# A decoder trunk in three-pass float32r: the shift product, the mean's copy, the diagonals, the merge's loop order and the last residual

## The chip, the cores and the metric

The program runs on 1 core of one Trainium2 chip. The metric is device microseconds of one execution, given as the median of three runs. Five engines matter: TensorE (PE, and PEld for its weight loads), VectorE (DVE), ScalarE (ACT), GpSimd (POOL), and SyncE (SP), which issues most DMAs.

## The reference, cut to what matters

Two layers; each has three steps, and each step ends in a layer norm over 1024 features. There are 528 tokens (16 learned meta tokens and 512 others), all in float32.

```
for l in range(2):
    h = layer_norm(ALPHA * h + 0.5 * swiglu(h, ffn1_w_up[l], ffn1_w_down[l]), ...)
    h = layer_norm(ALPHA * h + hybrid_mixer(h, ...), ...)
    h = layer_norm(ALPHA * h + 0.5 * swiglu(h, ffn2_w_up[l], ffn2_w_down[l]), ...)
return h[:, N_META:]
```

`swiglu` has 2816 hidden features. The mixer sums two gated branches, a short convolution and causal latent attention with 8 heads, and projects the sum by `w_o`.

## The kernel before, in words

**Products.** A float32 product runs as three float32r passes (`mm3`, L90 to L93): every operand is split into a rounded part and a rest. For weights ACT makes the rounded part (L111) and DVE the rest (L114); for activations both are in `split` (L88). Features lie on the partitions and tokens on the columns, so one pass takes 256, 264 or 272 columns.

**Token ranges and stages.** Tokens are cut in two parts, FULL (256 and 272) or, from the second layer's mixer on, TRIM (256 and 256 without the meta tokens). A feed-forward step (`ffn`) goes over pairs of feature tiles in chunks; `up_seven` makes two tiles of the hidden layer with seven products of halves, and calls `mid[...]` between them, which runs the down products of the chunk before (`down_features`). PSUM has eight banks: in a feed-forward step four for `psum()` (tile ps) and four for `psum2()` (tile pf), in the mixer six and two.

**What sets the order.** The kernel is written in the order of the generators' `yield`s and calls; the framework then orders each engine's instructions by its own estimate of when operands are ready. The order on an engine is fixed at compile time, and each engine takes its instructions strictly in that order. A block `tc.issue_after(ins)` puts what is issued in it behind `ins`, on the engine of `ins`.

**The norm.** `Norm.shift_by` (L248 to L257) takes the mean over the first 128 features of each token: DVE casts r's first tile to bf16 (L253), PE multiplies it by ones (L254), ACT copies the result (L256), and POOL subtracts it from r (L561 in the feed-forward step, L1133 in the merge). In `down_features` this happens within chunk 0, as soon as feature tile m = 0 of a part is added to r (L558). `Norm.add` (L259) collects sums of r and of its squares on DVE and POOL. `Norm.run` (L273) takes token sums on PE (L206), computes variance and `rsqrt` in 14 small DVE operations (L282 to L285 and L225 to L234), and spreads two rows over the partitions: `spread` (L210) makes diagonal matrices, by ACT for the mean (L216) and by DVE for the deviation (L218), and PE multiplies them by ones (L219). ACT copies the mean out of PSUM (L289), POOL subtracts it from r in eight operations (L292), DVE scales (L300), and ACT and DVE write the next operands xh and xl (L302 to L306, L88). There are five norms of two parts each that go this way; the mixer's two RMS norms use `spread` as well (`third`, L838), eight spreads in all.

**The merge.** `merge` (L1104) multiplies the two branches (w_bc with yc, w_bm with ym) for two feature tiles at a time, then projects by w_o, first for token part 0, then for part 1 (`proj_o`). Each product is followed by DVE operations (L1123, L1125) and a split into mg.

**The last residual.** In the last feed-forward step tokens go back to the partitions (`down_tokens`, L583). `begin` (L606) rebuilds x as xh + xl on DVE (L615), transposes it on PE (L617), and ACT writes it, scaled, to r viewed as four contiguous token tiles of 1024 (L618). It starts behind `combos` (L328), where POOL forms sums and differences of r (L337) that are split by ACT and DVE. `end` normalises (L647, L652), and SP stores 128 x 512 pieces (L654).

Of the kernel before, what the change touches and what calls it, by code (L numbers as in the profile page):

```python
# [51 lines left out]
def trunk(ctx: ExitStack, tc: tile.TileContext, x, meta, f1_up, f1_dn, w_in, b_gate, conv_w, qn_g, w_uq,  # L52
          kvn_g, w_ukv, w_bc, w_bm, w_o, f2_up, f2_dn, ln_g, ln_b, rope, out):
    """Float32 products run as three passes of float32r: an operand is hi + lo, hi its value rounded to 12
    significant bits and lo the exact rest, and hi*hi + hi*lo + lo*hi are summed in PSUM. Activations lie with
    their features on the partitions."""
# [8 lines left out]
    @contextmanager  # L65
    def scratch(n, t):
        """The eight banks of PSUM, n for psum() and the others for psum2(), and t tiles in SBUF."""
        with tc.tile_pool(name="psp", bufs=1, space=bass.MemoryType.PSUM, reuse_waits="tile") as pool, \
                tc.tile_pool(name="tmp", bufs=t, reuse_waits="tile") as tp:
            banks.append((pool, n))  # L70
            tps.append(tp)
            yield
            banks.pop()
            tps.pop()
# [15 lines left out]
    def mm3(ps, lhs, rhs, first, last, more=False):  # L90
        PE.matmul(ps, lhsT=lhs[0], rhs=rhs[0], start=first, stop=False, skip_group_check=more)  # L91
        PE.matmul(ps, lhsT=lhs[0], rhs=rhs[1], start=False, stop=False, skip_group_check=more)  # L92
        PE.matmul(ps, lhsT=lhs[1], rhs=rhs[0], start=False, stop=last, skip_group_check=more)  # L93
# [4 lines left out]
    def unit(pool=wp, k=8, c=P):  # L98
        """A stationary operand, hi and lo, as [128, k, c]."""
# [8 lines left out]
    def operand(raw, pool=wp, cut=1):  # L108
        """Split, in parts where others would wait for long."""
# [21 lines left out]
    # per-feature parameters as columns  # L131
# [11 lines left out]
    def tokens_in(xt, c0):  # L143
        """Two tiles of tokens, to the columns from c0."""
# [14 lines left out]
    with tc.tile_pool(name="xload", bufs=1, reuse_waits="tile") as xp, scratch(4, 1):  # L159
# [8 lines left out]
        # the array's clock falls while it waits for the first products' operands: of no use but for that  # L168
# [3 lines left out]
    def rest_in(pool):  # L172
        """The other tokens, and the parameters."""
# [21 lines left out]
    # Per-token statistics are taken with the tokens on the partitions, n of them in each of nt columns, and  # L195
    # spread back over the partitions of the features.
# [5 lines left out]
    def token_sums(ps, at, parts, n, nt):  # L202
        """Columns at, at + 2, ...: the means over D features of the parts together."""
# [6 lines left out]
    def spread(c, n, nt, act, ps):  # L210
        """c / D on all partitions."""
        ps = ps[:, :n * nt]
        for i in range(nt):
            dg = tmp(n)[0:n]
            if act:
                S.activation(dg, idf[0:n, 0:n], AF.Copy, scale=c[:, i:i + 1])  # L216
            else:
                V.tensor_scalar(dg, idf[0:n, 0:n], c[:, i:i + 1], None, op0=ALU.mult)  # L218
# [3 lines left out]
    def rsqrt(v, n, nt, by=float(D)):  # L222
        """by/sqrt(v): the exponent trick, a Newton step, and a step of third order."""
# [10 lines left out]
        V.tensor_tensor(y, u, y, op=ALU.mult)  # L234
        return y

    class Norm:
        """Layer norm over the features of r, which holds twice the sum to norm. The sums of r and of its squares
        are taken as its last parts come; by then r has been moved by a value near the mean of each token, which
        keeps the variance exact."""  # L240
# [7 lines left out]
        def shift_by(self, q0, w, i):  # L248
            """The mean of the first features of each token, on all partitions: near the mean, so that a rounded
            one does."""  # L250
            ps = psum()[:, :w]
            b = tmp(w).bitcast(BF16)[:, :w]
            V.tensor_copy(b, r[:, 0, q0:q0 + w])  # L253
            PE.matmul(ps, lhsT=onesb, rhs=b, start=True, stop=True)  # L254
            s = self.sums_tile(i, w)
            S.copy(s, ps)  # L256
            return s  # L257
# [15 lines left out]
        def run(self, q0, w):  # L273
            """The rest, in steps between which the tensor engine should have something else to do."""
# [11 lines left out]
            y = rsqrt(v, n, nt)  # L286
            yield
            mean = tmp(w)
            S.copy(mean, spread(mud, n, nt, True, psum2()))  # L289
# [4 lines left out]
            y = spread(y, n, nt, False, psum2())  # L294
# [24 lines left out]
    def project_steps(ps, u, nk, rhs, q0, w, n=4):  # L319
        """The same, with a stop after each n of the products' parts."""  # L320
# [7 lines left out]
    def combos(hv, th, tl):  # L328
        """Sums and differences of the parts of x (halves of its features, 1 and 2, and of its tokens, A and B)
        that the seven products take, split, from r that holds x. By index: T1 = x1B - x1A,  # L330
        T2 = x2B - T1, T3 = x2B - x1B, -T4 = x2A - T2."""
# [8 lines left out]
    def up_start(hp, dp, w_up, hv, pending, th, tl, after, begin):  # L340
        """silu(gate) * up for the first two pairs of feature tiles. What the first tokens allow comes first."""
# [62 lines left out]
    def up_seven(hp, fp, w_up, f, hv, mid, th, tl):  # L404
        """silu(gate) * up for two feature tiles by seven products of halves (Winograd's form): rows are gate and
        up, the contraction is halved, columns are the two token ranges."""
# [20 lines left out]
        product(pa, operand(g1), x1a, True)              # M1  # L427
# [28 lines left out]
        product(pc, operand(s1), t1, True)               # M5  # L456
        if mid[2]:
            mid[3]()
        for j in range(2):
            V.tensor_tensor(u3s[j], pc[j], u3s[j], op=ALU.add)   # up B  # L460
        if not mid[2]:
            mid[1]()
        product(pc, operand(g2, wp, 2), x2b, False)             # M5 + M3
        if mid[2]:
            mid[3]()
        for j in range(2):
            hh, hl = hs[j]
            V.tensor_tensor(u2s[j], pc[j], u2s[j], op=ALU.add)   # gate B
# [76 lines left out]
    def down_features(hv, norm):  # L545
        def down(ci, hs, mp, u, part):
            q0, w = hv[part]
            n = len(hs)
            for j in range(2):
# [3 lines left out]
                for k in range(n):  # L553
                    mm3(ps, [t[:, j * P:(j + 1) * P] for t in u[k]], [t[:, q0:q0 + w] for t in hs[k]],
                        k == 0, k == n - 1)
                if ci == 0:
                    rm = r[:, m, q0:q0 + w]
                    V.scalar_tensor_tensor(rm, rm, ALPHA2, ps, op0=ALU.mult, op1=ALU.add)  # L558
                    if m == 0:
                        shifts[part] = norm.shift_by(q0, w, part)  # L560
                    G.tensor_tensor(rm, rm, shifts[part], op=ALU.subtract)  # L561
# [17 lines left out]
        shifts = {}  # L579
# [3 lines left out]
    def down_tokens(l):  # L583
        """The last step's down products, with tokens on the partitions, and its norm."""
        rt = r.rearrange("p k t -> p (k t)")[:, 0:4 * D].rearrange("p (i d) -> p i d", d=D)

        def make(dp):
            state = {}

            def down(ci, hs, mp, u, part, tiles=None):  # L590
                last = ci == len(CHUNKS) - 1
                for i in tiles or (2 * part, 2 * part + 1):
# [5 lines left out]
                    rm = rt[:, i, mp * 256:(mp + 1) * 256]  # L598
                    V.tensor_tensor(rm, rm, ps, op=ALU.add)  # L599
# [6 lines left out]
            def begin():  # L606
                """The residual, token tile by token tile, where the features' x was."""
                for i in range(4):
                    t0 = META + i * P
                    for half in range(2):  # L610
                        ps = psum2()
                        for kk in range(4):
                            k = half * 4 + kk
                            xf = tmp(P)
                            V.tensor_tensor(xf, xh[:, k, t0:t0 + P].bitcast(F32),  # L615
                                            xl[:, k, t0:t0 + P].bitcast(F32), op=ALU.add)
                            PE.transpose(ps[:, kk * P:(kk + 1) * P], xf, idf)  # L617
                        S.activation(rt[:, i, half * 512:(half + 1) * 512], ps, AF.Copy, scale=ALPHA2)  # L618
# [17 lines left out]
            def end(tiles):  # L636
                """The norm of some tiles up to the scaling by the deviation, which is returned."""
# [6 lines left out]
                y = rsqrt(v, P, n, 1.0)  # L644
                halves = [(j, i, slice(c * 512, (c + 1) * 512)) for j, i in enumerate(tiles) for c in range(2)]
                for j, i, cs in halves:
                    V.scalar_tensor_tensor(rt[:, i, cs], rt[:, i, cs], mv[:, 2 * j:2 * j + 1], gb[0][:, cs],  # L647
                                           op0=ALU.subtract, op1=ALU.mult)

                def finish():  # L650
                    for j, i, cs in halves:
                        V.scalar_tensor_tensor(rt[:, i, cs], rt[:, i, cs], y[:, j:j + 1], gb[1][:, cs],  # L652
                                               op0=ALU.mult, op1=ALU.add)
                        nc.sync.dma_start(out[0, i * P:(i + 1) * P, cs], rt[:, i, cs])  # L654
# [19 lines left out]
    def gate(l, hv, wi, i, m2, dst, ps_of):  # L674
        """tanh of half the gates' arguments of two feature tiles: sigmoid(z) = (tanh(z / 2) + 1) / 2."""
# [523 lines left out]
```

## Time and profile before

| what | value |
|---|---|
| median of 3 runs | 2246.11 us (2245.96 to 2246.87) |
| profiled execution, span | 2247.7 us |
| PE busy / PEld busy | 2202.0 us (98%) / 2181.9 us (97%) |
| DVE / ACT / POOL busy | 1679.5 us (75%) / 974.5 us (43%) / 372.6 us (17%) |
| mean granted TensorE clock | 0.990 |

The profiled execution's own time is known by its span, from the first to the last instruction; it is 1.6 us above the median of the runs. Matmuls are pipelined: one is busy some 280 ns, and the next starts some 120 ns after it, so that the count of matmuls in a stretch tells more than the busy share.

### The profile page before, as it was taken

What the parts mean: (1) busy time and instruction counts of PE and PEld (TensorE: products, weight loads), DVE (VectorE), ACT (ScalarE), POOL (GpSimd) and SP (SyncE); (2) the same over time, 40 slices, a digit from 0 to 9 for tenths busy, and PEclk for the clock granted to TensorE, in tenths of its full rate; (3) what the DMA queues carried; (4) which work ended last, traced back from release to release, by engine and by line L of the source; (5) the groups of instructions that cost most, each with busy time, mean ns of one, the idle gap of its engine ahead of it and who ended that gap; (6) DMA issues with size and microseconds to landing.
All of it is one profiled execution on the core that took longest, in us unless ns stands there. A gap on an engine that the chain in (4) does not pass through costs nothing. (4 is left out here: it accounts for less than half of the span.)

```text
span 2247.7 us, 43950 instructions
## 1 busy us (share of the span) xinstructions
PE 2202.0 (98%) x17989; PEld 2181.9 (97%) x17989; DVE 1679.5 (75%) x3191; ACT 974.5 (43%) x1881; POOL 372.6 (17%) x487
## 2 busy tenths in 40 slices
PE   9999999999999999999999999999999999999998
PEld 8999999999999999999999999999999999999998
DVE  6777778876646777878778778787665568877887
ACT  4343344465533543434353433444655335443441
POOL 3210004211014512000242100042110155100000
PEclk9999999999999999999999999999999999999999
DMA  5232232222233223323323232322222332233322
GB/s 172 94 103 91 90 119 77 68 62 67 69 92 104 66 82 98 113 75 111 107 66 95 96 98 90 113 85 63 66 67 76 94 94 85 76 103 105 99 90 86
DMA packets 237418, 202.80 MB, mean 90 GB/s; under 512 B 6990, under 2 KB 233360, under 8 KB 237216
## 3 DMA queue, kind: packets, MB, share of 16 engines
q1 hardware_dynamic: 234880, 195.65, 28.2%
q0 software_dynamic: 2336, 4.34, 0.7%
q8 instruction: 141, 2.31, 0.4%
q14 instruction: 61, 0.50, 0.1%
HBM read 195.74 MB, written 2.10 MB: 88 GB/s over the span
## 5 line engine op out<-in xcount | busy, mean ns | idle before, releaser
L114 DVE TENSOR_TENSOR wl<-raw,wh 128x1024 fp32r<-128x1024 f32 (+1 forms) x490 | 560.5, 1145 | 250.0 <-ACT wh L111 248.5
L111 ACT CAST wh<-raw 128x1024 fp32r<-128x1024 f32 (+1 forms) x454 | 466.2, 1034 | 591.2 <-PE ps L92 174.3
L92 PE MATMUL ps<-xl,wh 128*128 128x256 f32 (+2 forms) x1760 | 501.7, 285 | 2.7 <-DVE xl L88 2.7
L91 PE MATMUL ps<-xh,wh 128*128 128x256 f32 (+2 forms) x1760 | 502.5, 286 | 0.1
L93 PE MATMUL ps<-xh,wl 128*128 128x256 f32 (+2 forms) x1760 | 501.6, 285 | 0.0
L92 PEld LDWEIGHTS ps<-xl,wh 128*128 128x128 f32 x1760 | 332.5, 189 | 4.3 <-DVE xl L88 4.0
L91 PEld LDWEIGHTS ps<-xh,wh 128*128 128x128 f32 x1760 | 333.0, 189 | 0.6 <-ACT xh L88 0.5
L93 PEld LDWEIGHTS ps<-xh,wl 128*128 128x128 f32 x1760 | 333.4, 189 | 0.0
L91 PE MATMUL ps<-th,wh 128*128 128x264 f32 (+1 forms) x1152 | 328.5, 285 | 0.0
L92 PE MATMUL ps<-tl,wh 128*128 128x264 f32 (+1 forms) x1152 | 327.6, 284 | 0.0
L93 PE MATMUL ps<-th,wl 128*128 128x264 f32 (+1 forms) x1152 | 326.9, 284 | 0.0
L91 PE MATMUL pf<-hh,wh 128*128 128x256 f32 (+1 forms) x864 | 246.7, 286 | 0.0
L93 PE MATMUL pf<-hh,wl 128*128 128x256 f32 (+1 forms) x864 | 246.3, 285 | 0.0
L92 PE MATMUL pf<-hl,wh 128*128 128x256 f32 (+1 forms) x864 | 245.3, 284 | 0.0
L92 PEld LDWEIGHTS ps<-tl,wh 128*128 128x128 f32 x1152 | 218.8, 190 | 0.0
L91 PEld LDWEIGHTS ps<-th,wh 128*128 128x128 f32 x1152 | 218.6, 190 | 0.1
L93 PEld LDWEIGHTS ps<-th,wl 128*128 128x128 f32 x1152 | 218.3, 189 | 0.0
L91 PE MATMUL pf<-xh,wh 128*128 128x256 f32 (+1 forms) x640 | 188.0, 294 | 0.0
L92 PE MATMUL pf<-xl,wh 128*128 128x256 f32 (+1 forms) x640 | 184.4, 288 | 0.0
L93 PE MATMUL pf<-xh,wl 128*128 128x256 f32 (+1 forms) x640 | 183.2, 286 | 0.0
L91 PEld LDWEIGHTS pf<-hh,wh 128*128 128x128 f32 x864 | 162.7, 188 | 0.0
L93 PEld LDWEIGHTS pf<-hh,wl 128*128 128x128 f32 x864 | 162.7, 188 | 0.0
(323 smaller groups left out, 4870.3 us busy)
## 6 DMA issues: line engine op xcount, KB each, us to landing
raw<-in_ffn_w_up_dram SPq DMA_DIRECT2D x176, 512.0 KB, 3.6
raw<-in_ffn_w_down_dram SPq DMA_DIRECT2D x80, 512.0 KB, 3.3
raw<-in_mix_w_in_dram SPq DMA_DIRECT2D x64, 512.0 KB, 3.7
raw<-in_w_o_dram SPq DMA_DIRECT2D x16, 512.0 KB, 3.9
raw<-in_ffn_w_down_dram SPq DMA_DIRECT2D x16, 256.0 KB, 2.6
raw<-in_w_br_conv_dram SPq DMA_DIRECT2D x8, 512.0 KB, 3.3
raw<-in_w_br_mla_dram SPq DMA_DIRECT2D x8, 512.0 KB, 3.3
out_dram<-r SPq DMA_DIRECT2D x8, 256.0 KB, 2.4
```

The lines of the kernel that those rows point to most:

```text
L91: PE.matmul(ps, lhsT=lhs[0], rhs=rhs[0], start=first, stop=False, skip_group_check=more)
L92: PE.matmul(ps, lhsT=lhs[0], rhs=rhs[1], start=False, stop=False, skip_group_check=more)
L93: PE.matmul(ps, lhsT=lhs[1], rhs=rhs[0], start=False, stop=last, skip_group_check=more)
L111: S.copy(u[0], raw)
L114: V.tensor_tensor(u[1][:, k:k + n], raw[:, k:k + n], u[0][:, k:k + n].bitcast(F32), op=ALU.subtract)
```

## The change

Five edits:

1. The shift in `down_features`: the bf16 cast stays behind feature tile m = 0; the product, ACT's copy and POOL's subtractions for m = 0, 1 and 2 come behind the last matmul of m = 2, which belongs to the next weight tile. In the merge the order is as before.
2. In `Norm.run` DVE copies the mean out of PSUM in place of ACT, and stands behind the last operation of `rsqrt` (L234).
3. All diagonals in `spread` are made by ACT.
4. The merge's products go by token part first, then by feature tile.
5. The last residual is transposed from r, which holds x, and written back in place, block by block; later operations on it and the stores use blocks of 128 columns.

Comments are removed as well.

```diff
-            if act:
-                S.activation(dg, idf[0:n, 0:n], AF.Copy, scale=c[:, i:i + 1])
-            else:
-                V.tensor_scalar(dg, idf[0:n, 0:n], c[:, i:i + 1], None, op0=ALU.mult)
+            S.activation(dg, idf[0:n, 0:n], AF.Copy, scale=c[:, i:i + 1])
...
-        V.tensor_tensor(y, u, y, op=ALU.mult)
-        return y
+        return y, V.tensor_tensor(y, u, y, op=ALU.mult)
...
-        def shift_by(self, q0, w, i):
-            ps = psum()[:, :w]
+        def shift_of(self, q0, w):
             b = tmp(w).bitcast(BF16)[:, :w]
             V.tensor_copy(b, r[:, 0, q0:q0 + w])
-            PE.matmul(ps, lhsT=onesb, rhs=b, start=True, stop=True)
-            s = self.sums_tile(i, w)
-            S.copy(s, ps)
-            return s
+
+            def shift(i):
+                ps = psum()[:, :w]
+                PE.matmul(ps, lhsT=onesb, rhs=b, start=True, stop=True)
+                s = self.sums_tile(i, w)
+                S.copy(s, ps)
+                return s
+
+            return shift
...
-            mean = tmp(w)
-            S.copy(mean, spread(mud, n, nt, True, psum2()))
+            mean, ps = tmp(w), spread(mud, n, nt, psum2())
+            with tc.issue_after(done.ins):
+                V.tensor_copy(mean, ps)
...
                     if m == 0:
-                        shifts[part] = norm.shift_by(q0, w, part)
-                    G.tensor_tensor(rm, rm, shifts[part], op=ALU.subtract)
+                        held[part] = norm.shift_of(q0, w)
+                    elif m == 2:
+                        with tc.issue_after(mm.ins):
+                            shifts[part] = held[part](part)
+                        for m1 in range(3):
+                            rm = r[:, m1, q0:q0 + w]
+                            G.tensor_tensor(rm, rm, shifts[part], op=ALU.subtract)
+                    elif m > 2:
+                        G.tensor_tensor(rm, rm, shifts[part], op=ALU.subtract)
...
-        rt = r.rearrange("p k t -> p (k t)")[:, 0:4 * D].rearrange("p (i d) -> p i d", d=D)
+        def rt(i, c0, c1):
+            return r[:, c0 // P:c1 // P, META + i * P:META + (i + 1) * P]
...
                         for kk in range(4):
-                            k = half * 4 + kk
-                            xf = tmp(P)
-                            V.tensor_tensor(xf, xh[:, k, t0:t0 + P].bitcast(F32),
-                                            xl[:, k, t0:t0 + P].bitcast(F32), op=ALU.add)
-                            PE.transpose(ps[:, kk * P:(kk + 1) * P], xf, idf)
-                        S.activation(rt[:, i, half * 512:(half + 1) * 512], ps, AF.Copy, scale=ALPHA2)
+                            PE.transpose(ps[:, kk * P:(kk + 1) * P], r[:, half * 4 + kk, t0:t0 + P], idf)
+                        S.activation(rt(i, half * 512, (half + 1) * 512), blocks(ps), AF.Copy, scale=ALPHA2)
...
-                        nc.sync.dma_start(out[0, i * P:(i + 1) * P, cs], rt[:, i, cs])
+                        nc.sync.dma_start(blocks(out[0, i * P:(i + 1) * P, cs]), ri)
...
-                for j in range(2):
-                    m = m2 + j
-                    for q0, w in hv:
+                for q0, w in hv:
+                    for j in range(2):
+                        m = m2 + j
```

## Rows read from the trace of the kernel before

**Rows 1.** The page's first part: busy time of each engine, share of the span.

```profile
PE 2202.0 (98%) x17989; PEld 2181.9 (97%) x17989; DVE 1679.5 (75%) x3191; ACT 974.5 (43%) x1881; POOL 372.6 (17%) x487
```

**Rows 2.** Who waited for whom, PE alone: us in total, times, longest us.

```profile
PE pf L219 <- DVE t L218: 11.1, 13, 1.9
PE ps L254 <- DVE t L253: 7.3, 3, 2.7
PE pf L617 <- DVE t L615: 3.4, 1, 3.4
...
PE ps L92 <- DVE mg L88: 2.8, 2, 2.0
PE ps L92 <- DVE xl L88: 2.7, 6, 0.7
```

**Rows 3.** Windows, PE alone: start:end, length, busy (matmuls), granted clock, DMA share, GB/s.

```profile
76.00:84.00 8.00, 5.27 (x33) 0.79 0.00 0
369.00:377.00 8.00, 5.83 (x34) 0.79 0.24 66
399.00:409.00 10.00, 8.21 (x53) 0.83 0.15 41
711.00:718.00 7.00, 4.97 (x29) 0.76 0.35 111
748.00:752.00 4.00, 3.06 (x23) 1.00 0.41 131
826.00:834.00 8.00, 5.57 (x33) 0.79 0.00 0
1119.00:1128.00 9.00, 6.87 (x42) 0.81 0.18 58
1201.00:1209.00 8.00, 5.73 (x35) 0.79 0.00 1
1494.00:1499.00 5.00, 2.79 (x21) 1.00 0.38 105
1523.00:1534.00 11.00, 9.44 (x51) 0.69 0.13 36
...
1920.00:1936.00 16.00, 12.59 (x86) 0.79 0.01 2
90.00:98.00 8.00, 8.00 (x67) 1.00 0.19 66
```

**Rows 4.** A window right behind the wait at 827: PE, PEld, DVE, ACT, POOL, clock, DMA.

```profile
830.20:833.60 3.40, 3.40 (x18) 3.40 (x17) 0.92 (x2) 1.69 (x3) 1.49 (x2) 0.50 0.00 0
```

**Rows 5.** Timeline of DVE in the first feed-forward step's chunk 0: start, us, instruction, [idle before].

```profile
75.67 1.23 DVE L431 TENSOR_TENSOR raw<-raw 128x1024 f32<-128x1024 f32 x1 [2.84 <-DMA raw<-in_ffn_w_up_dram]
...
78.97 0.82 DVE L253 CAST t<-r 128x272 bf16<-128x272 f32 x1
```

**Rows 6.** Timeline of DVE in `rsqrt`: with POOL's subtractions beside it, and at the end.

```profile
368.94 0.70 DVE L233 TENSOR_SCALAR sm<-sm 128x2 f32<-128x2 f32 x1
...
2242.89 0.15 DVE L233 TENSOR_SCALAR sm<-sm 128x1 f32<-128x1 f32 x1
```

**Rows 7.** Groups by line with shapes kept apart: count, busy, mean ns, idle before.

```profile
L216 ACT ACTIVATE t<-idf,sm 128x128 f32<-128x128 f32 x12 | 4.1, 392 | 0.4
L218 DVE TENSOR_SCALAR t<-idf,sm 128x128 f32<-128x128 f32 x20 | 8.8, 476 | 0.0
```

**Rows 8.** Line L216, who waited for it: us in total, times.

```profile
  PEld pf L219: 0.5, 2
```

**Rows 9.** Who waited for whom, ACT's casts of weights.

```profile
ACT wh L111 <- PE ps L92: 174.3, 143, 4.4
```

**Rows 10.** The page's DMA issues: count, KB each, us to landing.

```profile
raw<-in_ffn_w_up_dram SPq DMA_DIRECT2D x176, 512.0 KB, 3.6
...
raw<-in_w_o_dram SPq DMA_DIRECT2D x16, 512.0 KB, 3.9
...
out_dram<-r SPq DMA_DIRECT2D x8, 256.0 KB, 2.4
```

More of the change, by code (lines that the diff above doesn't have):

```diff
@@ L92, in mm3 @@
         PE.matmul(ps, lhsT=lhs[0], rhs=rhs[1], start=False, stop=False, skip_group_check=more)
-        PE.matmul(ps, lhsT=lhs[1], rhs=rhs[0], start=False, stop=last, skip_group_check=more)
+        return PE.matmul(ps, lhsT=lhs[1], rhs=rhs[0], start=False, stop=last, skip_group_check=more)
     def raw_tile(pool=rawp):
@@ L208, in token_sums, with spread @@
         return ps[0:n, at:at + 2 * nt].rearrange("p (i c) -> p i c", c=2)[:, :, 0]
-    def spread(c, n, nt, act, ps):
+    def spread(c, n, nt, ps):
         ps = ps[:, :n * nt]
@@ L285, in run @@
             V.scalar_tensor_tensor(v, ex2, LN_EPS4, v, op0=ALU.add, op1=ALU.subtract)
-            y = rsqrt(v, n, nt)
+            y, done = rsqrt(v, n, nt)
             yield
-            mean = tmp(w)
-            S.copy(mean, spread(mud, n, nt, True, psum2()))
+            mean, ps = tmp(w), spread(mud, n, nt, psum2())
+            with tc.issue_after(done.ins):
+                V.tensor_copy(mean, ps)
             for m in range(KD):
@@ L293, in run @@
             yield
-            y = spread(y, n, nt, False, psum2())
+            y = spread(y, n, nt, psum2())
             yield
@@ L553, in down @@
                 for k in range(n):
-                    mm3(ps, [t[:, j * P:(j + 1) * P] for t in u[k]], [t[:, q0:q0 + w] for t in hs[k]],
-                        k == 0, k == n - 1)
+                    mm = mm3(ps, [t[:, j * P:(j + 1) * P] for t in u[k]], [t[:, q0:q0 + w] for t in hs[k]],
+                             k == 0, k == n - 1)
                 if ci == 0:
@@ L578, in down_features @@
         state = {}
-        shifts = {}
+        shifts, held = {}, {}
         down.step, down.end, down.begin = step, end, lambda: iter(())
@@ L583, in down_tokens, with blocks @@
     def down_tokens(l):
-        rt = r.rearrange("p k t -> p (k t)")[:, 0:4 * D].rearrange("p (i d) -> p i d", d=D)
+        def rt(i, c0, c1):
+            return r[:, c0 // P:c1 // P, META + i * P:META + (i + 1) * P]
+        def blocks(t):
+            return t.rearrange("p (k c) -> p k c", c=P)
         def make(dp):
@@ L597, in down @@
                         mm3(ps, [t[:, t0:t0 + P] for t in hs[k]], u[k], k == 0, k == n - 1)
-                    rm = rt[:, i, mp * 256:(mp + 1) * 256]
-                    V.tensor_tensor(rm, rm, ps, op=ALU.add)
+                    rm = rt(i, mp * 256, (mp + 1) * 256)
+                    V.tensor_tensor(rm, rm, blocks(ps), op=ALU.add)
                     if last:
@@ L643, in end @@
                     V.tensor_scalar(v[:, j:j + 1], mv[:, 2 * j + 1:2 * j + 2], LN_EPS4, None, op0=ALU.add)
-                y = rsqrt(v, P, n, 1.0)
+                y = rsqrt(v, P, n, 1.0)[0]
                 halves = [(j, i, slice(c * 512, (c + 1) * 512)) for j, i in enumerate(tiles) for c in range(2)]
                 for j, i, cs in halves:
-                    V.scalar_tensor_tensor(rt[:, i, cs], rt[:, i, cs], mv[:, 2 * j:2 * j + 1], gb[0][:, cs],
+                    ri = rt(i, cs.start, cs.stop)
+                    V.scalar_tensor_tensor(ri, ri, mv[:, 2 * j:2 * j + 1], blocks(gb[0][:, cs]),
                                            op0=ALU.subtract, op1=ALU.mult)
@@ L651, in finish @@
                     for j, i, cs in halves:
-                        V.scalar_tensor_tensor(rt[:, i, cs], rt[:, i, cs], y[:, j:j + 1], gb[1][:, cs],
-                                               op0=ALU.mult, op1=ALU.add)
-                        nc.sync.dma_start(out[0, i * P:(i + 1) * P, cs], rt[:, i, cs])
+                        ri = rt(i, cs.start, cs.stop)
+                        V.scalar_tensor_tensor(ri, ri, y[:, j:j + 1], blocks(gb[1][:, cs]), op0=ALU.mult, op1=ALU.add)
+                        nc.sync.dma_start(blocks(out[0, i * P:(i + 1) * P, cs]), ri)
                 return finish
@@ L835, in second @@
                                     op0=ALU.mult, op1=ALU.add)
-                return rsqrt(v, n, 2 * nt)
+                return rsqrt(v, n, 2 * nt)[0]
             def third(part, res):
@@ L842, in third @@
                                         [(cq[j], QG + 2 * l + j, cqn[0][:, j], cqn[1][:, j]) for j in range(2)])):
-                    y = spread(res[:, i * nt:(i + 1) * nt], n, nt, False, psum())
+                    y = spread(res[:, i * nt:(i + 1) * nt], n, nt, psum())
                     for c, gi, hi, lo in of:
@@ L1128, in merge @@
             rm = add_x(0, q0, w, G)
-            s = norm.shift_by(q0, w, i)
+            s = norm.shift_of(q0, w)(i)
             for m in range(KD):
```

## The prediction

> **What bounds the kernel.** I read the page's busy times first: TensorE is busy 98% of the span, every other engine 75% or less [rows 1]. So only two things can shorten the kernel: fewer or faster products, of which the change has none, or fewer holes between them. The second view is PE's list of waits. Five waits carry the change: on the deviation's diagonals (L219, 11.1 us in 13), on the shift's cast (L254, 7.3 us in 3), on the rebuilt residual (L617, 3.4 us once), on the merge's split (2.8 us in 2), and on xl at the start of a feed-forward step (2.7 us in 6) [rows 2]. That list is too short as a price, because TensorE's clock falls behind a long wait: behind the one at 827 us it stands at 0.50, its lower level of 1.2 GHz, and 3.40 us hold 18 matmuls [rows 4]. The third view therefore counts matmuls in windows. An undisturbed 8.00 us hold 67 [rows 3], that is 0.119 us each; 3.40 us would hold 28.5, so one such stretch loses 10.5 x 0.119 = 1.25 us. A window's loss is its length less its matmuls times 0.119 us, and that holds wait and clock together.
>
> **The change part by part.** All sums are against the profiled execution's span of 2247.7 us; the median of the runs is 1.6 us less, and I subtract the gain from the median.
>
> *Shift.* The three windows hold 33, 33 and 35 matmuls in 8.00 us [rows 3]: 8.00 - 3.94 = 4.06, 4.06 and 3.82, together 11.9 us. The cause lies in DVE's order: the cast of the second part waits behind an operation that stood 2.84 us for a weight transfer (L431), and the cast itself takes 0.82 us at 78.97 [rows 5]; the product is next in PE's order. Moved behind feature tile m = 2 it comes a weight tile later, more than 24 matmuls on, and the cast is long done. What hides it is those products. ACT's copies and the number of POOL subtractions stay, in a burst of six. The bank is one of four in `psum()`, by then free but for two pairs, and the bf16 tile is held longer; I keep 0.3 us each for these: gain 11.0 us. Next late would be the operation that waited for the weights, which feeds only the pair after.
>
> *Diagonals and mean, feed-forward, part 0.* Windows with 34 in 8.00, 42 in 9.00 and 21 in 5.00 us [rows 3]: 3.94 + 3.99 + 2.49 = 10.4 us. Here two edits act together. Before, ACT copied the mean while `rsqrt` was still running, and POOL's subtractions slowed it: one operation takes 0.70 us beside them and 0.15 us alone [rows 6]. With the copy behind L234 the three last operations are alone, 3 x 0.55 = 1.65 us earlier; the diagonal then takes 392 ns on ACT instead of 476 on DVE [rows 7], without DVE's other work in front. The wait of at most 1.9 us [rows 2] shrinks to a few tenths; the window at 748, which lost 1.25 us, kept its clock at 1.00 [rows 3], so the clock should stay up here too. I leave 0.6 us per place: gain 8.6 us. Bounds: 0 if the last operations stay late, 10.4 if all goes.
>
> A rule speaks against this edit: the Trainium skill, "ScalarE: Activation LUTs", section "Rules for kernel authors", sends multiplications to VectorE and not to ScalarE. The trace differs: 476 ns on DVE, 392 on ACT for the same shape [rows 7], since DVE's are made beside POOL's work. By the rule the difference of 0.084 us would be turned round, and the 18 moved spreads would cost 18 x 0.17 = 3 us against the sum below.
>
> *The same, in the mixer (part 1).* Windows with 53 in 10.00 and 51 in 11.00 us [rows 3]: 3.67 + 4.91 = 8.6 us. There the deviation is ready early, but DVE has an operation for the RMS norm, which waits for PE's own sums, in front of the diagonals. ACT isn't tied to that. Gain 6.6, leaving 1.0 each, since the part that follows needs POOL's subtractions too.
>
> *The same, in the merge.* 23 in 4.00 us [rows 3]: 1.25 us; gain 1.0. Its smaller repeat in the second layer is left out. The eight RMS spreads move as well; their waits were near zero and I keep them so.
>
> *Against these:* ACT had 28 diagonals, gets 52 more, and DVE gets ten copies for the 52; neither engine is near full [rows 1]. At the three starts of a feed-forward step (xl) the mean may leave DVE later than it left ACT: 2.7 us of waits there [rows 2]; I add 0.5 us in all, between 0 and 3.
>
> *Merge by token range.* 29 in 7.00 us [rows 3]: 3.54 us in the first layer, and 2.8 - 2.0 = 0.8 us in the second [rows 2]. The last split that `proj_o` needs for part 0 was third of four in DVE's line and becomes second, one product of 12 x 0.119 = 1.4 us earlier. DVE remains full of splits, slowed by POOL, so I take 3.0 of 4.3. Bounds 0 and 4.3.
>
> *Last residual.* 86 in 16.00 us [rows 3]: 16.00 - 10.27 = 5.7 us. PE waited 3.4 us for the first DVE addition [rows 2], which stood behind the splits of `combos`. r holds x already, so the transposes need no DVE work. ACT's writes must still wait until POOL has read r, and four banks hold only half of the transposes; I take 4.2. Bounds 0 and 5.7.
>
> *Stores.* The pieces on the chip's side shrink from 2 KB to 512 B. The nearest rows are loads of 512 KB: 3.6 us in pieces of 1 KB and 3.9 us in 512 B [rows 10]; half of that size costs about 0.15 us more on the last store's 2.4 us. I take 0.2, bounds 0 and 0.5.
>
> Sum: 11.0 + 8.6 + 6.6 + 1.0 + 3.0 + 4.2 - 0.5 - 0.2 = 33.7 us, of 42.3 that the windows hold. 2246.1 - 33.7 = **2212 us**.
>
> **The rivals.**
>
> *The contention is moved, not removed.* POOL does the same subtractions, only later, beside DVE's scaling and splitting. If `rsqrt` gains nothing because DVE's weight splits stand between its operations, the norm's part halves (-8.1), and if the late mean shows at the starts of the steps, 2 us more: gain 23.6, 2222 us. For it: DVE is the second busiest engine [rows 1], and an operation takes over four times as long beside POOL [rows 6]. Against: xh and xl of part 0 are needed only after part 1's last down products. The Trainium skill, "SBUF — State Buffer", section "Who interferes with whom", says that a VectorE instruction with two SBUF inputs contends with GpSimd's reads, and one that reads PSUM alone doesn't; by that the scalings (one SBUF tile, one PSUM tile) would escape, the splits not. The trace [rows 6] shows the slowdown for a one-input operation of a kind that the page lists as contending too. I give it 0.20.
>
> *The shift meets the next wait.* If DVE's lateness comes back to PE at the next bank or operand, the 11.0 us go and the rest stays: 2223 us. For it: the 2.84 us wait of DVE for weights isn't touched [rows 5]. Against: PE works on with operands split before. 0.10.
>
> *Slower: ACT as a new gate.* ACT takes its diagonals in order, and its weight casts wait for PE to free a buffer, 174.3 us in 143 waits, 1.2 us each, up to 4.4 [rows 9]. If each of the 18 moved spreads stands behind such a cast, PE loses 18 x 1.2 = 22 us, and with a clock stretch of 1.25 us behind a third of them 7 us more: 29 us, while the norm's 16.2 us are not gained. The other terms bring 17.5, so the kernel is 12 us slower: 2258 us. It decides from a wait of 1.0 us per spread on. Against: the 28 diagonals that ACT makes already cost PE 0.5 us in all [rows 8]. 0.04.
>
> *The change doesn't do what it says.* The order on each engine comes from estimates at compile time; if PE meets the spreads, the merge and the transposes with the same delays as before, only a few us move: 2243 us. 0.04.
>
> **How the numbers follow.** A measurement of this kernel can tell about 0.2% (4.5 us) from no change. The forecast, 2205 to 2219 us, has 0.62; with the two lesser gains, faster by over 0.2% has 0.92, within it 0.04, slower 0.04. The range reaches from nearly all of the 42.3 us (2203) past the two lesser gains to a case in which both cost something (2229).
>
> **What would show it.** Right: L254 and L617 leave PE's list of waits; L219 waits under 3 us in all; the granted clock in the windows named stands at 1.00, and each holds as many matmuls as an undisturbed one; operations of `rsqrt` at about 0.16 us throughout; POOL's subtractions start behind L234. Wrong: ACT's L216 high in PE's list, or new waits on xl, mg or banks of several us; a mean clock no higher than 0.990.

## The result, and the profile after

The changed kernel takes 2213.24 us (median of 4 runs, 2211.29 to 2215.05) against 2246.49 us (2245.96 to 2248.0) before: a ratio of 0.9853, with an interval of 0.9839 to 0.9867. That is 33 us faster, where 34 had been forecast (2212 us, range 2203 to 2229). The profiled execution has a span of 2213.0 us; before it was 2247.7, so the two traces differ by 34.7 us.

The page's busy line, which answers to [rows 1], and the stores' line of its DMA issues, which answers to the last of [rows 10]:

```profile
PE 2185.1 (99%) x17989; PEld 2166.9 (98%) x17989; DVE 1663.6 (75%) x3117; ACT 984.7 (44%) x1923; POOL 369.6 (17%) x487
...
out_dram<-r SPq DMA_DIRECT2D x8, 256.0 KB, 2.5
```

TensorE does the same 17989 products and is busy 16.9 us less: its mean granted clock rose from 0.990 to 0.998, and 0.8% of the span is 17.7 us. The rest of the gain is idle time that went. VectorE, 75% before, is at 75% still.

PE's list of waits after (us in total, times, longest), which answers to [rows 2]:

```profile
PE ps L91 <- DVE r L572: 5.0, 3, 1.8
...
PE ps L92 <- DVE xl L88: 2.8, 6, 0.8
...
PE pf L216 <- ACT t L215: 1.3, 2, 0.6
PE ps L91 <- DVE t L447: 1.2, 2, 0.7
```

The line numbers have shifted by a few: the spread's product is L216 now (L219 before), its diagonal L215, the shift's product L252 (L254 before), the additions of the down products L572 (L564 before). Four of the five waits that the prediction named are gone or small: L254, L617 and mg are not in the list, and the diagonals cost 1.3 us in 2 waits in place of 11.1 in 13. The waits on xl are what they were. At the top stands a wait that the list of before doesn't have: 5.0 us in 3, on VectorE's additions L572.

Windows of PE alone (start:end, length, busy and matmuls, granted clock, DMA share, GB/s), laid where the work of [rows 3] now stands:

```profile
78.00:86.00 8.00, 7.48 (x62) 1.00 0.21 68
815.00:823.00 8.00, 8.00 (x67) 1.00 0.22 68
1184.00:1192.00 8.00, 7.35 (x61) 1.00 0.21 67
365.00:373.00 8.00, 8.00 (x64) 1.00 0.28 74
378.00:386.00 8.00, 6.13 (x55) 1.00 0.30 73
1101.00:1109.00 8.00, 8.00 (x64) 1.00 0.22 67
1113.00:1122.00 9.00, 7.21 (x55) 0.81 0.39 118
1469.00:1477.00 8.00, 7.97 (x64) 1.00 0.48 131
1484.00:1490.00 6.00, 4.26 (x34) 1.00 0.00 0
394.00:404.00 10.00, 9.36 (x80) 1.00 0.14 41
1501.00:1511.00 10.00, 9.36 (x80) 1.00 0.15 41
736.00:740.00 4.00, 4.00 (x32) 1.00 0.75 207
703.00:710.00 7.00, 7.00 (x61) 1.00 0.52 152
1892.00:1908.00 16.00, 16.00 (x140) 1.00 0.40 122
```

The prediction's measure, length less 0.119 us per matmul, gives a small table (a value below zero counts as 0):

| part | lost before | lost after | gain | forecast | gain by the same product |
|---|---|---|---|---|---|
| shift (first three windows) | 11.9 | 0.6 + 0 + 0.7 = 1.4 | 10.5 | 11.0 | 10.8 |
| end of a feed-forward step, part 0 (next six) | 10.4 | 0.4 + 1.5 + 0.4 + 2.5 + 0.4 + 2.0 = 7.0 | 3.4 | 8.6 | 2.8 |
| mixer, part 1 (394, 1501) | 8.6 | 0.5 + 0.5 = 1.0 | 7.6 | 6.6 | 7.9 |
| merge's norm (736) | 1.25 | 0.2 | 1.1 | 1.0 | 1.2 |
| merge by token range (703, and mg in the second layer) | 4.3 | 0 | 4.3 | 3.0 | 4.8 |
| last residual (1892) | 5.7 | 0 | 5.7 | 4.2 | 6.4 |

The gains by windows make 32.6 us of the span's 34.7; the forecast was 34.4 for these lines, less 0.7 for the starts of the feed-forward steps and the stores, which cost about 0.1 us each. The last column is a second measure, which doesn't depend on where a window is laid: both kernels run 17989 products, in the same order but for the pieces that were moved, so the start of the product with the same number is compared in the two traces, at both ends of each part. These gains make 33.9 us, and 0.9 more is the merge's norm in the second layer, which the prediction left out. The total came out nearly as summed, then, and its parts didn't: one term brought well under half, and three others brought more.

**Where the missing gain sits.** VectorE's timeline at the first feed-forward step's end (start, us, instruction), the last operations of `rsqrt` to the mean's copy L290:

```profile
364.87 0.16 DVE L230 TENSOR_SCALAR sm<-sm 128x2 f32<-128x2 f32 x1
...
365.28 0.15 DVE L231 TENSOR_TENSOR sm<-sm 128x2 f32<-128x2 f32 x1
365.35 0.41 DVE L290 COPY t<-pf 128x256 f32<-128x256 f32 x1
```

Here the forecast holds: the operation that took 0.70 us [rows 6], now L230, takes 0.16, because POOL starts later (e2 below has it the other way). POOL's eight subtractions begin at 365.85 and last 6.37 us (first line below); 12 us on, VectorE is still catching up, as the next lines of its timeline show, and PE's line below them has the price:

```profile
365.85 6.37 POOL L293 TENSOR_TENSOR r<-r,t 128x256 f32<-128x256 f32 x8 [8.30 <-ACT hh L88]
...
378.45 0.43 DVE L270 TENSOR_TENSOR rs<-rs,r 128x272 f32<-128x272 f32 x1
378.81 0.97 DVE L307 SCALAR_TENSOR_TENSOR xl<-r,prm,xh 128x256 fp32r<-128x256 f32 x1
379.70 0.42 DVE L572 TENSOR_TENSOR r<-r,ps 128x272 f32<-128x272 f32 x1
...
380.27 0.35 PE L91 MATMUL ps<-xh,wh 128*128 128x256 f32 x1 [1.59 <-DVE r L572]
```

VectorE has no gap in front of these operations from 368.2 us on. PE's first product of the mixer needs the PSUM bank that L572 empties; L572 stands in VectorE's line behind the norm's scalings of part 0 (L301), its splits (L307) and the sums of part 1 (L270). Before, PE itself came some 4 us late to this point [rows 3], and VectorE had that time: it stood idle for 2.0 us of the same stretch.

### The profile page after: what moved, and what is told of

It reads as the page before. It is cut to its first block, busy times and chain, and to the rows that moved or that the text cites. A ratio compares the mean times of both kernels' runs of the same rounds, so it can differ in the third digit from the quotient of the medians.

```text
span 2213.0 us, 43882 instructions
## 1 busy us (share of the span) xinstructions
PE 2185.1 (99%) x17989; PEld 2166.9 (98%) x17989; DVE 1663.6 (75%) x3117; ACT 984.7 (44%) x1923; POOL 369.6 (17%) x487
```

## The experiments

The kernels e1 to e4 ran on one chip, e5 to e8 on another, e9 to e11 on a third, each set with the kernel before beside it (2247.10, 2245.08 and 2246.24 us). Ratios are against that. The changed kernel ran again as e8.

### Each edit undone

**e1: the shift back behind feature tile 0**, with the rest of the change kept.

```diff
-                        held[part] = norm.shift_of(q0, w)
-                    elif m == 2:
...
+                        shifts[part] = norm.shift_of(q0, w)(part)
+                    G.tensor_tensor(rm, rm, shifts[part], op=ALU.subtract)
```

> The changed kernel (2213.2 us), with the shift's product, its copy and the subtractions back behind feature tile m = 0; the other four edits stay. Theory, the shift pays by itself: the three waits of PE on the bf16 cast come back (7 us in all), each with a stretch at clock 0.50, and the kernel takes about 2213 + 11.5 = 2225 us. Rival, what the shift gives is taken back at the end of each feed-forward step, where PE now waits for VectorE's last additions (L572, 5.0 us in 3): then those waits shrink here by 4 to 5 us and the kernel takes 2219 us or less.

Measured: 2223.55 us, ratio 0.9907 (0.9887 to 0.9927). Against the changed kernel's ratio that is 0.0054 or 12 us, with some 5 us either way. PE's wait on the cast is back, and L572 is as in the changed kernel:

```profile
PE ps L252 <- DVE t L248: 7.7, 3, 2.8
PE ps L91 <- DVE r L565: 5.0, 3, 1.8
```

So the shift's term stands by itself. Windows of PE around its three waits (2.8, 2.2 and 2.8 us long) show something else:

```profile
75.00:83.00 8.00, 5.17 (x30) 0.79 0.00 0
814.50:822.50 8.00, 5.77 (x47) 1.00 0.00 1
1185.50:1193.50 8.00, 5.18 (x42) 1.00 0.01 2
```

Only the first wait was followed by the lower clock in this execution; in [rows 3] all three were. The third has the busy time of the first (5.18 us against 5.17), and 12 matmuls more.

**e2: the mean copied by ACT, as before**, with the diagonals on ACT.

```diff
-            with tc.issue_after(done.ins):
-                V.tensor_copy(mean, ps)
+            S.copy(mean, ps)
```

> The changed kernel with the mean copied by ScalarE as before, with nothing to hold it behind the deviation's operations; all diagonals stay with ScalarE. Theory, contention moved: GpSimd's subtractions start some 2 us earlier, slow the last operations of rsqrt (0.7 in place of 0.16 us each), and are over sooner, so that the waits on the last additions (5.0 us in 3) fall below 2.5 us, while waits on diagonals come back by about as much: 2211 to 2216 us. Rival, contention removed: the waits on the last additions stay at 5 us, those on diagonals come back with 2 us at each of three steps and their clock: 2219 to 2223 us.

Measured: 2211.07 us, ratio 0.9848 (0.9832 to 0.9865), no slower than the changed kernel. PE's list has the wait at the other place, and no L572:

```profile
PE pf L216 <- ACT t L215: 5.4, 5, 1.4
```

VectorE's timeline shows the slow operations of `rsqrt` again, here the last two, and the addition that has the place of the one PE waits for in the changed kernel:

```profile
364.61 0.70 DVE L230 TENSOR_SCALAR sm<-sm 128x2 f32<-128x2 f32 x1
...
365.57 0.68 DVE L231 TENSOR_TENSOR sm<-sm 128x2 f32<-128x2 f32 x1
...
378.76 0.42 DVE L571 TENSOR_TENSOR r<-r,ps 128x272 f32<-128x272 f32 x1
```

From the end of `rsqrt` to the end of that addition VectorE takes 12.9 us here (366.25 to 379.18), and 14.7 us in the changed kernel (365.43 to 380.12); at the other two steps' ends it is 12.9 against 14.8 and 12.9 against 14.7. POOL's subtractions run beside this stretch for 3.8 us here and for 6.6 us there, and VectorE's splits of xl in it have these means, first here, then in the changed kernel:

```profile
L306 DVE SCALAR_TENSOR_TENSOR xl<-r,prm,xh 128x256 fp32r<-128x256 f32 x8 | 5.2, 667 | 0.0
...
L307 DVE SCALAR_TENSOR_TENSOR xl<-r,prm,xh 128x256 fp32r<-128x256 f32 x7 | 5.6, 812 | 0.0
```

The late copy does to `rsqrt` what was forecast, and it buys nothing: 5.4 us of waits on the deviation become 1.3 there and 5.0 on the last additions. This is the prediction's rival, contention moved and not removed, for this one edit.

**e3: the diagonals of the deviations and of the RMS norms back on VectorE**, the mean's on ACT and its copy late, as in the changed kernel.

```diff
-            S.activation(dg, idf[0:n, 0:n], AF.Copy, scale=c[:, i:i + 1])
+            if act:
+                S.activation(dg, idf[0:n, 0:n], AF.Copy, scale=c[:, i:i + 1])
+            else:
+                V.tensor_scalar(dg, idf[0:n, 0:n], c[:, i:i + 1], None, op0=ALU.mult)
```

> The changed kernel with the deviation's and the RMS norms' diagonals back on VectorE; the mean's copy stays with VectorE behind the deviation's operations. Theory, the engine of the diagonals is what pays in the mixer and the merge: waits of PE on diagonals come back there with 4 to 5 us and two stretches at clock 0.50 in the mixer, 2221 to 2224 us. Rival, the freed rsqrt alone pays: waits on diagonals stay under 2 us, 2212 to 2215 us.

Measured: 2223.61 us, ratio 0.9905 (0.9888 to 0.9922), 10.4 us above the changed kernel by the medians. PE's waits, and the group of VectorE's diagonals:

```profile
PE pf L219 <- DVE t L218: 5.6, 12, 1.0
```

```profile
L218 DVE TENSOR_SCALAR t<-idf,sm 128x128 f32<-128x128 f32 x20 | 9.9, 544 | 0.0
```

Three of the twenty, at 419 us, where POOL's subtractions don't run:

```profile
L218 DVE TENSOR_SCALAR t<-idf,sm 128x128 f32<-128x128 f32 x3 | 0.7, 279 | 0.0
```

One window of its first mixer shows what came with the waits:

```profile
395.00:405.00 10.00, 9.46 (x49) 0.66 0.01 2
```

It lost 4.2 us, more than the 3.67 of [rows 3] and against 0.5 in the changed kernel. In the mixers the norm's gain comes from the diagonals' engine: by the same products they take 7.1 us longer here than in the changed kernel. At the ends of the feed-forward steps it doesn't show: this kernel keeps 2.9 us there, as much as the changed one (2.8). The rule that the prediction weighed (the Trainium skill, "ScalarE: Activation LUTs", "Rules for kernel authors": multiplications belong on VectorE) doesn't decide here. The trace agrees with it where POOL's subtractions don't run, 279 ns on VectorE for a tile that takes 392 on ACT [rows 7]; but beside POOL the tile takes up to 790 ns, the mean is 544, and VectorE's queue comes on top.

**e4: the merge in its old order.**

```diff
-                for q0, w in hv:
-                    for j in range(2):
-                        m = m2 + j
+                for j in range(2):
+                    m = m2 + j
+                    for q0, w in hv:
```

> The changed kernel with the merge's products in the old order, feature tile first. Theory, the order alone removed the wait on the split of the last feature tile: it comes back with 2.0 and 0.8 us and one stretch at half clock, 2217 to 2219 us. Rival, PE's other timing had removed it: no wait on mg over 0.5 us, 2212 to 2215 us.

Measured: 2216.48 us, ratio 0.9872 (0.9854 to 0.9891). The difference of 3 to 4 us lies within the intervals; the trace carries the verdict, where both waits on the merge's split are back (2.0 us in the first layer, 0.8 in the second). By the same products the two merges take 3.3 us longer than in the changed kernel.

```profile
PE ps L92 <- DVE mg L88: 2.8, 2, 2.0
```

**e5: the last residual and the stores as before.**

```diff
-                            PE.transpose(ps[:, kk * P:(kk + 1) * P], r[:, half * 4 + kk, t0:t0 + P], idf)
+                            k = half * 4 + kk
+                            xf = tmp(P)
+                            V.tensor_tensor(xf, xh[:, k, t0:t0 + P].bitcast(F32),
+                                            xl[:, k, t0:t0 + P].bitcast(F32), op=ALU.add)
+                            PE.transpose(ps[:, kk * P:(kk + 1) * P], xf, idf)
```

> The changed kernel with the last residual as it was: x rebuilt from xh and xl on VectorE, r as four contiguous token tiles, stores in pieces of 2 KB. Theory, the missing VectorE additions are the gain: PE waits some 3.4 us for the first of them, with a stretch at half clock behind it, the last store lands within 0.2 us of the changed kernel's, and the kernel takes 4 to 6.5 us more than the changed one. Rival, the wait was due to combos and to ScalarE: it is there in the changed kernel's other places too, and this kernel takes within 2 us of it.

Measured: 2218.16 us (2217.03 to 2218.49), ratio 0.9875 (0.9858 to 0.9891). The changed kernel on the same chip, e8, took 2212.86 (2210.56 to 2213.51): 5.3 us. The one long wait is back:

```profile
PE pf L625 <- DVE t L623: 3.4, 1, 3.4
```

**e8: the changed kernel once more**, as the measure for e5 to e7.

> The changed kernel once more, beside the kernels of this group, as their reference: 2211 to 2215 us by every theory; the same waits of PE as before on the last additions (5.0 us in 3).

Measured: 2212.86 us, ratio 0.9851 (0.9837 to 0.9866), with the waits of the first trace (L572 5.1 us in 3).

### What stands behind the new wait

**e6: other banks.** In the first feed-forward step of each layer the two kinds of PSUM banks are exchanged, so that the mixer's first product doesn't need the bank that the last additions empty. One theory: the bank is the cause, and the wait goes. The rival: VectorE is late as a whole, and PE meets it at the next operand.

```diff
-            banks.append((pool, n))
+            banks.append(((pool0, pool1)[::-1] if flip else (pool0, pool1), n))
...
-        pool, n = banks[-1]
+        (_, pool), n = banks[-1]
...
-                scratch(*FFN_SCR):
+                scratch(*FFN_SCR, flip=idx % 3 == 0):
```

> The changed kernel with the PSUM banks of the first feed-forward step of each layer exchanged, so that the next stage's first products and those after the second feed-forward step land in banks that the last down products did not use; the instructions are the same. Theory, the bank is what PE waits for at the end of a feed-forward step: the wait on L572 (5.0 us in 3) goes, 5 us faster than the changed kernel. Rival, VectorE is behind with all its work there: PE then waits for xl in the product that it may now begin (2 us or more in place of 0.5 us on L307), within 2 us of the changed kernel.

Measured: 2220.06 us, ratio 0.9884 (0.9869 to 0.9899), 7.2 us slower than e8. L572 is gone from PE's list; others took its place:

```profile
PE ps L93 <- DVE xl L308: 3.8, 2, 1.9
PE ps L93 <- DVE xl L89: 3.5, 7, 0.8
```

The waits on xl at the starts of the steps grew from 2.8 us in 6 to 3.5 in 7, and the norm's own xl (L308) took the bank's place. The bank is where VectorE's lateness shows, not its cause. Not all of the 7.2 us belong to the banks. The two traces differ by 10.7 us, and by the same products 4.4 of these lie in the first 20 us, where PE waits 2.7 us for a transfer of x (L149) that it doesn't wait for in e8; 3.9 us lie at the ends of the feed-forward steps, waits and clock together (mean clock 0.996 against 0.998). Whether the start is due to the edit is open.

**e7: the deviation's spread one step later**, from e2, to give `rsqrt` more time before PE comes to it.

```diff
-            y = spread(y, n, nt, psum2())
             yield
+            y = spread(y, n, nt, psum2())
```

> The kernel of the second experiment (mean copied by ScalarE, not held back; all diagonals by ScalarE; 2211.1 us) with the deviation's spread asked for one step later, so that some of the last down products run in front of it. Theory, PE only comes too early to the spread: its waits on ScalarE's diagonals (5.4 us in 5) fall by 2 to 4 us and nothing comes in their place, 2207 to 2209 us. Rival, VectorE and GpSimd set the end of the step: the same time comes back as a wait on xl or on the last additions, 2210 to 2213 us.

Measured: 2226.46 us (2221.44 to 2229.17), ratio 0.9911 (0.9894 to 0.9928), worse than either theory had it. The wait at L216 fell to 1.3 us; what depends on the deviation came later still:

```profile
PE ps L92 <- DVE xl L88: 5.6, 11, 1.5
...
PE ps L92 <- DVE xl L306: 2.9, 2, 1.5
```

**e9: less work for VectorE.** The changed kernel without VectorE's additions of tiles 2 to 7 to the sum of r, in three of the feed-forward steps' norms; the means there are of two tiles alone, and nothing else is left out.

```diff
-                V.tensor_tensor(s2, s, rm, op=ALU.add)
+                if m == 1 or self.idx % 3 == 1:
+                    V.tensor_tensor(s2, s, rm, op=ALU.add)
```

> The changed kernel without VectorE's additions of feature tiles 2 to 7 to the sum of r in the three feed-forward norms (36 operations of some 0.4 us and more left out, so the means and the output are wrong); everything else as it was. Theory, VectorE is behind at the end of a feed-forward step: with less work there the wait on the last additions (5.0 us in 3) falls below 1.5 us, no wait on xl takes its place, and the kernel takes 2205 to 2209 us. Rival, what PE waits for there is GpSimd's or ScalarE's share of the norm: the wait stays above 3.5 us or comes back on xl, 2211 to 2214 us.

Measured: 2207.90 us (2207.35 to 2208.33), ratio 0.9831 (0.9818 to 0.9845), some 5 us below the changed kernel, with intervals that meet. The wait on the last additions is halved, from 5.0, and not gone:

```profile
PE ps L91 <- DVE r L573: 2.4, 3, 1.3
```

These additions are 12 of 0.43 us in a step, half of them for part 1, which stand in the stretch in front of the last L572; taking them away moves L572 forward. That VectorE is behind there is shown, and that the sums are only part of it. (By the same products, what is lost there against the kernel before falls from 7.2 us, or 5.7 in e8, to 1.4.)

**e10: the order of VectorE's work.** From e2: the splits of the next stage's first weights are held behind `rsqrt`'s last operation, so that no 1.2 us operation stands between `rsqrt`'s own.

```diff
+                elif roots:
+                    with tc.issue_after(roots[-1].ins):
+                        us.append(operand(raw, pool))
...
-        ukv = columns(wi, C_KV)
+        with tc.issue_after(roots[-1].ins):
+            ukv = columns(wi, C_KV)
```

> The kernel of the second experiment (mean copied by ScalarE, 2211.1 us) with the next stage's first weight splits held behind the deviation's last operation on VectorE, in whose gaps they stood. Theory, at the end of a feed-forward step PE waits for the deviation (4.2 of its 5.4 us of waits on diagonals): that falls below 1.5 us, and the kernel takes 2206 to 2209 us, faster than both. Rival, the delayed splits and the scaling then come as late as before: waits on xl, on wl or on the last additions of 3 us or more in its place, 2210 to 2214 us.

Measured: 2209.64 us (5 runs, 2205.95 to 2210.68), ratio 0.9833 (0.9819 to 0.9846). It is the fastest of the complete kernels, some 4 us below the changed one, but its interval meets that of the changed kernel (0.9839 to 0.9867), so that a step forward is likely and not proved. The wait on the deviation fell from 5.4 us to 1.3, and smaller ones came up:

```profile
PE ps L92 <- DVE hl L88: 2.1, 3, 1.0
PE pf L216 <- ACT t L215: 1.3, 2, 0.6
...
PE pf L206 <- POOL rq L274: 0.9, 1, 0.9
```

### One edit alone

**e11: the kernel before with all diagonals on ACT**, and nothing else of the change.

```diff
-            if act:
-                S.activation(dg, idf[0:n, 0:n], AF.Copy, scale=c[:, i:i + 1])
-            else:
-                V.tensor_scalar(dg, idf[0:n, 0:n], c[:, i:i + 1], None, op0=ALU.mult)
+            S.activation(dg, idf[0:n, 0:n], AF.Copy, scale=c[:, i:i + 1])
```

> The kernel before with one edit alone: all diagonals by ScalarE. Theory, this edit carries nearly the whole gain of the norm's part (16.2 us forecast; the reverse experiment cost 10 to 11 us): 2246 - 10 = 2236 us, 2233 to 2238. Rival, it pays only together with the other edits, which make PE arrive earlier: 2240 us or more.

Measured: 2231.57 us, ratio 0.9939 (0.9925 to 0.9952), 14.7 us faster than before by the medians and a little more than expected. PE's wait for the shift is untouched, and the deviation's has ACT as its releaser; the windows are those of the first feed-forward step's end and of the two mixers:

```profile
PE ps L251 <- DVE t L250: 8.1, 3, 2.8
PE pf L216 <- ACT t L215: 5.4, 5, 1.4
```

```profile
368.00:376.00 8.00, 6.62 (x53) 1.00 0.40 114
...
397.00:407.00 10.00, 9.36 (x81) 1.00 0.14 41
1513.00:1524.00 11.00, 10.36 (x89) 1.00 0.15 44
```

Without the late copy the mixers lose 0.4 us each instead of 3.67 and 4.91, and the first feed-forward step's end 1.7 instead of 3.94. The whole gain of the norm is this one edit, and more: its three lines of the table make 12.1 us with all five edits together. At the ends of the feed-forward steps it brings 5.3 us by the same products, against 2.8 in the changed kernel (4.4 in e8). The sum over the parts comes near: 14.7 (e11), 10.3 (e1 by the medians), 3.2 (e4) and 5.3 (e5) make 33.5 us, and the late copy takes some 2 back (e2), which leaves 31 of the 33 measured. Each of these differences carries some us either way, the last above all, whose interval meets the changed kernel's; what shows the late copy's cost is the trace of e2.

## Why the prediction was right, and where not

**What bounds the kernel: right.** TensorE's holes were the only currency, and counting matmuls in windows priced wait and clock together. The lists of waits alone would have given 11.1 + 7.3 + 3.4 + 2.8 = 24.6 us for the four that went, of which 5.0 came back.

**Shift: right**, 10.5 us for 11.0. The rival that it meets the next wait, which would have taken all 11, took the small remainder: PE waits on L447, 1.2 us in 2, at about 80 and 1187 us. L447 stands in VectorE's line behind the operation that the prediction named as late next (now L432), which waited 3.34 and 3.48 us for its weights there; in e8 it waited 2.70 us at the first place, and PE's wait on L447 isn't in the list.

**Diagonals and mean at the feed-forward steps' ends: the step that failed.** The prediction put 8.6 us here, of 10.4; the windows give 3.4, the same products 2.8 (4.4 in e8, where the lower clock didn't follow). It said that two edits act together, and that the late copy makes the deviation earlier by 1.65 us. That happened, and the wait at the spread went. What failed is the sentence that the wait would shrink to a few tenths and leave nothing behind. PE met the lateness again some 12 us later, at the additions L572, three times 1.6 to 1.8 us. The late copy moves POOL's subtractions from `rsqrt` to VectorE's splits behind it: the stretch from `rsqrt` to that addition takes 14.7 us with hardly a gap, and 12.9 where ACT copies at once, in e2 and in e11. These 1.8 us are about the size of each wait. (Before, the same stretch took 14.7 us at the first step's end, 2.0 of them idle, and PE came late itself.) So the copy as such gains nothing (e2); the bank is not the cause (e6); and less work for VectorE shortens the wait (e9). The prediction did name this mechanism as its first rival, at 2222 us. The mechanism came true for this place, and the price was less than the rival's: the mixer, which the rival halved as well, wasn't touched by it, and the starts of the steps cost 0.1 us and not 2.

The last operations of `rsqrt` took 0.68 and 0.70 us beside POOL in e2 and 0.15 and 0.16 in the changed kernel, and the time of the kernel didn't follow them, since the queue behind them grew by about as much (1.8 us). On L231, which has two inputs in SBUF, the trace agrees with the Trainium skill, "SBUF — State Buffer", "Who interferes with whom", by which such an instruction of VectorE contends with one of GpSimd that reads SBUF. What the prediction drew from that section for its first rival came true as well: the splits, with two inputs in SBUF, became slower (812 ns against 667 in e2), and the scalings L301, with one tile in SBUF, didn't (471 against 473).

**Diagonals in the mixer: right in mechanism, undersized**, 7.6 for 6.6. A residue of 1.0 us per place had been kept for POOL's part; it is 0.5. **Merge by token range** (4.3 for 3.0) **and last residual** (5.7 for 4.2) were held below their windows for fear of VectorE's splits and of four banks; neither showed, and the windows hold an undisturbed number of matmuls. These three undersized terms, 3.8 us in all, and 2 us that lie outside the windows hid the oversized one, 5.2 us. That the total came out within 2 us was luck to that extent: the errors of the terms had opposite signs.

**ACT as a new gate: it wasn't.** That rival needed 1.0 us at each of 18 spreads; L216 waits for ACT 1.3 us in all, in 2 places.

**The signs.** Of those given for right, the granted clock stands at 1.00 in all windows but one (0.81 at 1113), and the mean is 0.998; L254 and L617 left the list, and the deviation's spread waits 1.3 us, under the 3 that were given. The windows behind the new wait don't hold what an undisturbed one does (55 matmuls in 8.00 us, 34 in 6.00). Of those given for wrong, one came: a new wait of several us, on a bank. It was a sign for one term, not for the total.

## What to carry to other kernels

When PE waits for a small tile from an engine that has a long queue, ask whether the edit shortens that queue or only reorders it: moving the diagonals to another engine took work off VectorE and stayed gained, moving the mean's copy reordered VectorE's and POOL's work, and the wait returned at the next thing VectorE owed. Price a wait by the matmuls missing in a window around it, and after the change look at the same stage up to the end of the queue, not only at the line that was mended. An edit that takes an engine out of a chain altogether (the residual from r, with no addition ahead of it) brought its full window here.

## What the runs showed of the hardware

The lower clock follows only some of the waits that look alike. Before, all three waits for the shift were followed by it [rows 3]; in e1, with waits of 2.2 to 2.8 us there, one of three was, in the execution that was profiled; the three others had a mean clock of 0.996 against 0.998 and took 2.6 to 5.0 us longer. In the changed kernel one of the three waits on L572 was, at the second step's end (1.8 us, behind which the clock stood at 0.50 as in [rows 4]), as the window of all engines shows:

```profile
1116.70:1120.10 3.40, 3.40 (x18) 3.40 (x17) 1.27 (x4) 0.43 (x1) 1.56 (x2) 0.50 0.95 297
```

In e8, the same kernel, none was; by the same products, what that end loses against the kernel before is 2.1 us there and 3.6 in the first trace. The spans were 2208.5 and 2213.0 us. In e10, on the other hand, the clock fell at 383.5 us, a microsecond behind a wait of only 0.9 us (the L206 of its list, whose products have two columns):

```profile
383.50:387.00 3.50, 3.50 (x19) 3.50 (x18) 3.12 (x12) 2.95 (x6) 3.44 (x9) 0.52 1.00 293
```

A single profile can therefore put a clock stretch on a wait or leave it out, by these two traces 1.5 us (the prediction's count from [rows 4] gave 1.25). What decides between them was not tested.

Left open: the waits on xl at the starts of the feed-forward steps (2.7 us in 6 before, 2.8 after, 2.7 in e10), which no kernel here was made to shorten, and a complete kernel that takes VectorE's sums off the feed-forward steps' ends, which wasn't tried.
